# A decoder trunk on one core: when the attention units of a head pair are started beside the projections of the next pair

## The chip, the core and the metric

The kernel runs on one core of a Trainium2 chip. The metric is the device time of one execution in microseconds; for the kernel before three runs were timed, and one more execution was profiled. The names of the engines are those of the profile: PE (TensorE matmuls), PEld (its weight loads), DVE (VectorE), ACT (ScalarE), POOL (GpSimd), SP (SyncE, which issues all transfers spoken of here). One microsecond of TensorE's time is spent, in most of the kernel, on fp32 products made of three fp32r products each.

## What is computed

Two layers over 1024 tokens of width 1024 (float32): the first mixes tokens with a forgetting attention of 16 heads of 64, the second with a convolution, and each is followed by a gated feed-forward net of width 2816 with a short convolution. The change touches the attention of the first layer alone, which is, cut to its core:

```python
proj = h @ w_in                                   # q, k, v and one gate logit per head
log_f = jax.nn.log_sigmoid(proj[..., 3 * d:] + b_f)
cum = jnp.cumsum(log_f, axis=1)                   # per head, over tokens
q, k = rms_norm(q, q_g), rms_norm(k, k_g)         # over the 64 of a head
for i in range(s // 128):                         # causal
    logits = q[i] @ k[:i+1].T / sqrt(64) + cum[i][:, None] - cum[:i+1][None, :]
    p = softmax(where(kpos <= qpos, logits, -inf))
    out[i] = p @ v[:i+1]
x = x + concat(out) @ w_o
```

## The kernel before

The heads are worked through in 8 pairs, p = 0 to 7. For a pair, `project` (L801) runs over 8 blocks t of 128 tokens: 24 matmuls of 128x384 into a PSUM tile `pj` (two buffers), which give the block's q, k and v of both heads. `mm3` (L349 to L355) makes each product of three (hi by hi, lo by hi, hi by lo), from halves that `split` (L345) makes: the hi by a cast on ACT (L346), the lo by a subtraction on POOL, or DVE (L347). The block is then copied out (L816 and L819 on ACT, L820 on DVE, the last reader of `pj`), its sums of squares go through ACT, DVE (L826) and POOL (L169, L170), q and k are scaled (L831, DVE) and transposed on PE (`qkT`, L836). After each second block, a chunk of 256 tokens is split into sq, kd, kl (L842 to L851), and copies on SP's queue (L853) bring the halves to the other partitions. These tiles lie in a pool of 22 buffers, 16 of them for one pair.

A unit of attention is one head and one group g of 256 query tokens. Its first half (`softmax_rows`, L885) computes scores on PE (L897 to L900), adds the gate term and takes the minimum on DVE (L904), the exponential on ACT (L910), the reciprocal on DVE (L911) and the scaling on POOL (L912). Its second half (`weigh_values`, L916) transposes on PE (`pT`, L926), splits (ACT L933, DVE L934) and multiplies by v into `ov` (L938, L939), which ACT and DVE add up in `of` (L943, L944). When both heads of a group are through, `finish_unit` (L948) writes the 128 columns' hi and lo: straight into the operand of w_o if that lies in SBUF already (ACT L955 and DVE L956, on 128x128, twice), or else through `ohi` (ACT L960) and `olo` (POOL L961) and stores on SP (L966) to memory, from where `fetch` (L998) brings them back. `fetch(hf, k0, k1)` brings pairs k0 to k1-1 for the half hf of the tokens (512 each), and makes that half's operand tiles.

A pair has eight units; groups run from 3 down to 0 (short units last), in the last pair from 0 up to 3. `step()` takes the next unit from the list `pend`, writes its first half, and the second half of the unit before it. In the loop over pairs and blocks (L1013 to L1043) one `step()` follows each block, so that the units of pair p-1 lie beside the projections of pair p; the last pair's eight units follow when its projections are written. A fetch of the first half stands behind block 4 of the last pair. After the last pair the pool of the projection weights is closed, and `early` loads w_o: three slices of 512 KB into the space of that pool (`wohi`, `wolo`: L1049, L346, L347 of 128x1024), then three more into the pool of 22. Then comes the fetch of the second half, and the remaining units.

A scheduler behind the language moves instructions among each other, with priority by the order in which they are written; so the order on an engine is not that of the source, and each engine then works through its own order without skipping. The product with w_o (`attn_out`, L1064; PSUM tile `wops`) is moved in between the last units in this way.

Of the kernel before, what the change touches and what calls it, by code (L numbers as in the profile page):

```python
# [22 lines left out]
KT = D // P  # L23
# [6 lines left out]
def f32(ap):  # L30
    return ap.bitcast(F32)
# [17 lines left out]


N_POOL = 10
ROW_BUFS = 8
GATES = (2, 1)
BEAT = (3.3, 3.6)
# [58 lines left out]
class Trunk:  # L113
# [21 lines left out]
    def rows_to_cols(self, pool, psum, tag, dst, rows, later=None):  # L135
# [3 lines left out]
        tot = sum(r.shape[0] for r in rows)  # L139
        t = pool.tile([P, P], F32, tag="rows", name=self.n("rows"), bufs=ROW_BUFS)  # L140
        o = 0
# [561 lines left out]
    def attn(self, wst0, x_in, gain, w_in, b_f, q_g, k_g, extra=lambda *a: None, early=lambda: None):  # L703
        nc, tc = self.nc, self.tc
        W = 3 * P + NH
        with ExitStack() as st:
# [20 lines left out]
            def load_w(p, q):  # L727

                wid = W if p == 0 else 3 * P
                hi, lo, raw = (  # L730
                    wp.tile([P, 2 * W + 32], dt, tag=m, name=self.n(m), bufs=n)[:, : 2 * wid].rearrange(
                        "p (k n) -> p k n", k=2
                    )
                    for m, dt, n in (("whi", F32R, WIN_BUFS), ("wlo", F32R, WIN_BUFS), ("raw", F32, 2))
                )
                ks = slice(2 * q, 2 * q + 2)
                for j in range(2):
                    qkv = wv[:, 2 * q + j, : 3 * D].rearrange("p (s n) -> p s n", s=3)
                    nc.sync.dma_start(
                        raw[:, j, : 3 * P].rearrange("p (s n) -> p s n", s=3), qkv[:, :, p * P : (p + 1) * P]  # L740
                    )
                if p == 0:
                    nc.sync.dma_start(raw[:, :, 3 * P : W], wv[:, ks, 3 * D : 3 * D + NH])
                self.split(hi[:, :, :wid], lo[:, :, :wid], raw[:, :, :wid], p == 0)
                return hi, lo
# [33 lines left out]
            for a in range(2):  # L779
                t = cp.tile([P, 512], F32R, name=f"ptd{a}")  # L780
# [5 lines left out]
            def load_norm(t):  # L786
                xt = first[t] if t < 2 else load_x(t)
                self.norm_block(xp, pss, "s", xt, self.to_split_as_is(ht[t // 4]), t, "x", gains=[grow])
# [3 lines left out]
            def new_pair(p):  # L792
                pairs[p] = []
# [154 lines left out]
            def finish_unit(p, g, ofull):  # L948

                if g // 2 in ot:  # L950
                    for e in range(2):
                        i = 2 * g + 1 - e
                        c = slice((i % 4) * P, (i % 4 + 1) * P)
                        hi, lo = (m.at(p)[:, c] for m in ot[g // 2])
                        nc.scalar.copy(hi, ofull[:, e, :])  # L955
                        nc.vector.tensor_tensor(lo, ofull[:, e, :], f32(hi), op=ALU.subtract)  # L956
                else:
                    hi = sp.tile([P, 2, P], F32R, tag="ohi", name=self.n("ohi"), bufs=1)
                    lo = sp.tile([P, 2, P], F32R, tag="olo", name=self.n("olo"), bufs=1)
                    nc.scalar.copy(hi, ofull)  # L960
                    nc.gpsimd.tensor_tensor(lo, ofull, f32(hi), op=ALU.subtract)  # L961

                    for e in range(2):
                        i = 2 * g + 1 - e
                        for a, t in ((0, hi), (1, lo)):
                            nc.sync.dma_start(otd[a][p, :, i * P : (i + 1) * P], f32(t[:, e, :]))  # L966

            def attn_units(p):
                st = {}

                def first(g, h):
                    if h not in st:
                        nct = xp.tile([P, S], F32, tag="nct", name=self.n("nct"), bufs=NC_BUFS)
                        nc.sync.dma_start(nct, ncd[2 * p + h : 2 * p + h + 1, :].partition_broadcast(P))
                        st[h] = nct
                    st[g, h] = softmax_rows(p, h, g, st[h])

                def second(g, h):
                    if h == 0:
                        st["of", g] = sp.tile([P, 2, P], F32, tag="of", name=self.n("of"))  # L980
                    weigh_values(p, h, g, st[g, h], st["of", g])
                    if h == 1:
                        finish_unit(p, g, st["of", g])

                gs = range(4) if p == KT - 1 else range(3, -1, -1)
                return [(lambda g=g, h=h: first(g, h), lambda g=g, h=h: second(g, h)) for g in gs for h in range(2)]

            pend = []
            late = []

            def fetch(hf, k0, k1):

                if hf not in ot:
                    ot[hf] = self.ht_half(hf)
                for q in range(2):
                    j0, j1 = max(k0, 4 * q), min(k1, 4 * q + 4)
                    for a in range(2 if j0 < j1 else 0):
                        nc.sync.dma_start(  # L998
                            f32(ot[hf][a].q[q][:, j0 - 4 * q : j1 - 4 * q, :]),
                            otd[a][j0:j1, :, hf * 512 : (hf + 1) * 512].rearrange("k p s -> p k s"),  # L1000
                        )

            def step():

                if pend:
                    a, b = pend.pop(0)
                    a()
                    late.append(b)
                    if len(late) > 1:
                        late.pop(0)()  # L1010
                elif late:
                    late.pop(0)()

            for p in range(KT):
                if p == 0:
                    load_norm(0)
                ws = [load_w(p, q) for q in range(KT // 2)] if p else w_first + [load_w(0, q) for q in range(1, KT // 2)]
                new_pair(p)
                if p == 0:
                    load_norm(1)  # L1020
                for t in range(NB):
                    project(p, ws, t)
                    step()
                    if p == 0 and t + 2 < NB:
                        load_norm(t + 2)
                    if p == KT - 1 and t == 4:
                        fetch(0, 0, KT - 2)
                    if p == 0 and t == NB - 1:
                        tables = extra(sp, ptr, "tr")
                    if p == 1 and t >= 4:  # L1030
                        for _ in range(2):
                            if tables:
                                tables.pop(0)()
                if p == 0:
                    cum()
                pend += attn_units(p)
            wst.close()
            early()
            fetch(1, 0, KT - 2)
# [67 lines left out]
    def conv(self, xs, xd, h, ht, w_pw1, los, taps, vec, w_pw2, halo, after):  # L1107
# [4 lines left out]
        H = C - 1  # L1112
        n_pool = N_POOL
        wv = w_pw1.rearrange("(k p) n -> p k n", p=P)
# [475 lines left out]
```

## Time and profile before

| | us |
|---|---|
| three timed runs | 2339.28, 2334.06, 2335.76 |
| their median | 2335.76 |
| the profiled execution | 2333.51 |
| its span | 2331.8 |
| PE busy from 30 to 515 (projections with attention) | 474.33 of 485 |
| PE busy from 515 to 600 (the last units, first of w_o) | 75.44 of 85 |
| PE busy from 600 to 1000 | 394.00 of 400 |

The span is the time between the first and the last instruction of the profiled execution; the execution's own time is 1.71 us longer. In a row of a timeline, the bracket says how long the engine sat idle before and which instruction released it. In a table of stretches, the busy time of each engine stands with the number of its instructions, and PEclk is the clock granted to TensorE as a share of full speed.

### The profile page before, as it was taken

What the parts mean: (1) busy time and instruction counts of PE and PEld (TensorE: products, weight loads), DVE (VectorE), ACT (ScalarE), POOL (GpSimd) and SP (SyncE); (2) the same over time, 40 slices, a digit from 0 to 9 for tenths busy, and PEclk for the clock granted to TensorE, in tenths of its full rate; (3) what the DMA queues carried; (4) which work ended last, traced back from release to release, by engine and by line L of the source; (5) the groups of instructions that cost most, each with busy time, mean ns of one, the idle gap of its engine ahead of it and who ended that gap; (6) DMA issues with size and microseconds to landing.
All of it is one profiled execution on the core that took longest, in us unless ns stands there. A gap on an engine that the chain in (4) does not pass through costs nothing.

```text
span 2331.8 us, 35304 instructions
## 1 busy us (share of the span) xinstructions
PE 2253.5 (97%) x11282; PEld 1927.3 (83%) x11282; DVE 1650.9 (71%) x2751; ACT 1355.8 (58%) x2832; POOL 1403.7 (60%) x1188
## 2 busy tenths in 40 slices
PE   7899999998999999999999999998899999999998
PEld 7899999997878887777787887777687788888887
DVE  5567777777368999998436995699539999983322
ACT  5567667667255666666445665566535666664443
POOL 3355455535018988885554886677425999955453
PEclk9999999999999999999999999999999999999999
DMA  5222222144256456666888767664454455466664
GB/s 145 65 78 83 78 78 78 56 130 141 80 180 191 154 157 205 201 200 198 301 257 288 257 218 270 205 185 144 147 193 157 150 157 154 147 228 206 219 204 153
DMA packets 366841, 392.63 MB, mean 168 GB/s; under 512 B 26416, under 2 KB 245312, under 8 KB 366656
## 3 DMA queue, kind: packets, MB, share of 16 engines
q1 hardware_dynamic: 366656, 390.38, 52.8%
q8 instruction: 89, 1.46, 0.3%
q14 instruction: 96, 0.79, 0.1%
HBM read 299.78 MB, written 82.12 MB: 164 GB/s over the span
## 4 chain that ended last, share of the span: by engine, by line
PE 49%; DVE 15%; issue 4%; ACT 4%; DMA 2%; POOL 1%; SPq 0%; DVEq 0%; ACTq 0%; POOLq 0%
DVE acc L578 8%; PE dn L353 7%; PE dn L352 7%; PE dn L354 7%; PE pw L352 2%; PE pw L353 2%; PE pw L354 2%; PE y L352 2%; PE e L352 2%; PE e L354 2%; PE e L353 2%; PE y L353 2%; PE y L354 2%; ACT acc L582 1%; PE z L352 1%
## 5 line engine op out<-in xcount | busy, mean ns | idle before, releaser
L347 POOL TENSOR_TENSOR wlo<-raw,whi 128x512 fp32r<-128x512 f32 (+1 forms) x306 | 444.3, 1454 | 285.3 <-ACT whi L346 254.3
L346 ACT CAST whi<-raw 128x512 fp32r<-128x512 f32 (+2 forms) x497 | 303.2, 633 | 268.2 <-PE dn L353 154.8
L347 DVE TENSOR_TENSOR wlo<-raw,whi 128x512 fp32r<-128x512 f32 (+1 forms) x191 | 149.3, 785 | 229.8 <-ACT whi L346 214.3
L347 POOL TENSOR_TENSOR wlo<-s,whi 128x512 fp32r<-128x512 f32 x176 | 258.4, 1479 | 63.8 <-ACT whi L346 63.8
L352 PE MATMUL dn<-whi,whi 128*128 128x512 f32 x704 | 275.5, 391 | 1.2 <-ACT whi L346 0.7
L353 PE MATMUL dn<-wlo,whi 128*128 128x512 f32 x704 | 274.6, 390 | 0.8 <-POOL wlo L347 0.8
L354 PE MATMUL dn<-whi,wlo 128*128 128x512 f32 x704 | 274.4, 390 | 0.0
L1174 DVE SCALAR_TENSOR_TENSOR cacc<-u,ctaps,cacc 128x512 f32<-128x512 f32 x320 | 238.6, 754 | 9.0
L1179 POOL TENSOR_TENSOR pacc<-pacc,prod 128x512 f32<-128x512 f32 x144 | 188.7, 1313 | 50.3 <-ACT prod L1178 43.4
L352 PE MATMUL y<-bhi,whi 128*128 128x512 f32 x528 | 207.7, 393 | 7.6 <-DVE u L636 5.0
L354 PE MATMUL y<-bhi,wlo 128*128 128x512 f32 x528 | 205.7, 390 | 0.0
L353 PE MATMUL y<-blo,whi 128*128 128x512 f32 x528 | 205.6, 389 | 0.0
L169 POOL TENSOR_SCALAR ss<-ss 128x4 f32<-128x4 f32 (+1 forms) x96 | 22.6, 235 | 291.5 <-ACT hn L189 150.7
L352 PE MATMUL pj<-whi,hthi 128*128 128x384 f32 (+1 forms) x512 | 178.3, 349 | 5.1 <-DVE zf L822 1.9
L354 PE MATMUL pj<-whi,htlo 128*128 128x384 f32 (+1 forms) x512 | 177.9, 348 | 0.0
L353 PE MATMUL pj<-wlo,hthi 128*128 128x384 f32 (+1 forms) x512 | 176.8, 346 | 0.7 <-DVE wlo L347 0.7
L912 POOL TENSOR_SCALAR x<-x,nm 128x896 f32<-128x896 f32 (+7 forms) x128 | 101.0, 794 | 106.3 <-DVE nm L911 74.6
L556 POOL TENSOR_TENSOR s<-raw,raw 128x512 f32<-128x512 f32 x88 | 126.4, 1437 | 62.6 <-DMA c11d<-ev 57.4
L352 PEld LDWEIGHTS dn<-whi,whi 128*128 128x128 f32 x704 | 132.6, 188 | 29.5 <-ACT whi L346 1.2
L353 PEld LDWEIGHTS dn<-wlo,whi 128*128 128x128 f32 x704 | 132.4, 188 | 28.8 <-POOL wlo L347 1.2
L354 PEld LDWEIGHTS dn<-whi,wlo 128*128 128x128 f32 x704 | 132.4, 188 | 27.7
L582 ACT ACTIVATE acc<-acc 128x512 f32<-128x512 f32 x88 | 55.7, 633 | 164.3 <-DVE acc L578 163.0
(221 smaller groups left out, 6411.1 us busy)
## 6 DMA issues: line engine op xcount, KB each, us to landing
raw<-in_ffn_w_up_dram SPq DMA_DIRECT2D x240, 256.0 KB
raw<-in_ffn_w_down_dram SPq DMA_DIRECT2D x176, 256.0 KB
raw<-actd SPq DMA_DIRECT2D x152, 256.0 KB
raw<-in_conv_w_pw_dram SPq DMA_DIRECT2D x96, 256.0 KB
actd<-acc SPq DMA_DIRECT2D x76, 256.0 KB
wlo<-pwlo SPq DMA_DIRECT2D x64, 256.0 KB
raw<-in_fox_w_in_dram SPq DMA_DIRECT2D x64, 192.0 KB
xd<-x SPq DMA_DIRECT2D x24, 512.0 KB
```

The costliest lines, as they stand in the source:

```text
L169: nc.gpsimd.tensor_scalar(ss, ss, 1.0 / n, EPS, op0=ALU.mult, op1=ALU.add)
L346: self.nc.scalar.copy(hi, raw)
L347: (self.nc.vector if vector else self.nc.gpsimd).tensor_tensor(lo, raw, f32(hi), op=ALU.subtract)
L352: nc.tensor.matmul(out, lh, rh, start=start, stop=False, skip_group_check=more)
L353: nc.tensor.matmul(out, lh, rl, start=False, stop=False, skip_group_check=more)
L354: nc.tensor.matmul(out, ll, rh, start=False, stop=stop, skip_group_check=more)
L556: nc.gpsimd.tensor_tensor(st[o], *(st[m].rearrange("p a b -> p (a b)") if m[0] == "a" else st[m] for m in ((y, x) if o == "s4" else (x, y) ...
L578: nc.vector.scalar_tensor_tensor(acc[:, j:], ps[:, : 512 - j], tap[2 - j], acc[:, j:], op0=ALU.mult, op1=ALU.add)
L582: nc.scalar.activation(acc, acc, AF.Silu)
L912: nc.gpsimd.tensor_scalar(X[:, :L], X[:, :L], nm[:, 2:3], 1.0, op0=ALU.mult, op1=ALU.mult)
L1174: nc.vector.scalar_tensor_tensor(acc, win(j), tap(j), acc, op0=ALU.mult, op1=ALU.add)
L1179: nc.gpsimd.tensor_tensor(pacc, pacc, p, op=ALU.add)
```

## The change

A table `STEPS` says how many `step()` calls follow a block: none at blocks 0 and 1 of pair 1, two at its blocks 4 and 6, two at blocks 0 to 3 of the last pair, one elsewhere. So the eight units of pair 6 are written beside four blocks of pair 7. At block 4 of the last pair, its own units enter the list, and four of them (groups 0 and 1) follow blocks 4 to 7; four remain behind the projections. The fetch of the first half at block 4 now covers pairs 0 to 6, since pair 6 is written to memory altogether.

```diff
@@ -49,6 +49,7 @@
 N_POOL = 10
+STEPS = {(1, 0): 0, (1, 1): 0, (1, 4): 2, (1, 6): 2}
 ROW_BUFS = 8
@@ -1020,11 +1021,14 @@
                 for t in range(NB):
                     project(p, ws, t)
-                    step()
+                    if p == KT - 1 and t == 4:
+                        pend += attn_units(p)
+                    for _ in range(STEPS.get((p, t), 2 if p == KT - 1 and t < 4 else 1)):
+                        step()
                     if p == 0 and t + 2 < NB:
                         load_norm(t + 2)
                     if p == KT - 1 and t == 4:
-                        fetch(0, 0, KT - 2)
+                        fetch(0, 0, KT - 1)
@@ -1033,7 +1037,8 @@
                 if p == 0:
                     cum()
-                pend += attn_units(p)
+                if p < KT - 1:
+                    pend += attn_units(p)
             wst.close()
             early()
             fetch(1, 0, KT - 2)
```

Line numbers of the changed kernel are one higher from L53 on, and five higher from L1042 on (L347 becomes L348, L1049 becomes L1054).

What this does to the orders is shown at three places. The first is PE's order at the last pair's block 6 (`pj_7083` before, `pj_7250` in the change; `pj_6978` is the block before it; s are scores and pT transposes of pair 6). Before:

```order
L926 MATMUL pT_6701<-ident,x_6510 128x128
L353 MATMUL pj_6978<-wlo_6350,hthi_13_144 128x384
L354 MATMUL pj_6978<-whi_6349,htlo_15_146 128x384
L352 MATMUL pj_6978<-whi_6349,hthi_13_144 128x384
L353 MATMUL pj_6978<-wlo_6350,hthi_13_144 128x384
L354 MATMUL pj_6978<-whi_6349,htlo_15_146 128x384
L352 MATMUL pj_7083<-whi_6328,hthi_12_143 128x384
L353 MATMUL pj_7083<-wlo_6329,hthi_12_143 128x384
```

In the change:

```order
L927 MATMUL pT_6857<-ident,x_6691 128x128
L927 MATMUL pT_6857<-ident,x_6707 128x128
L898 MATMUL s_6990<-kd_5433,sq_5432 128x256
L899 MATMUL s_6990<-kl_5434,sq_5432 128x256
L901 LDWEIGHTS identb
L901 MATMUL s_6990<-maskt,identb 128x128
L353 MATMUL pj_7250<-whi_6328,hthi_12_143 128x384
L354 MATMUL pj_7250<-wlo_6329,hthi_12_143 128x384
```

Block 6 followed block 5's matmuls directly; in the change the 48 matmuls ahead of it (from the four transposes `qkT` of the second chunk on) are all of attention, and blocks 4 and 5 stand before those.

The second place is SP's order around the first loads of w_o (`raw`, from in_fox_w_o_dram). Before:

```order
L998 DMA hthi_1457_7308<-otd_103 128x4x512
L998 DMA htlo_1459_7310<-otd_104 128x4x512
L998 DMA hthi_1458_7309<-otd_103 128x2x512
L1049 DMA raw_7260<-in_fox_w_o_dram 128x1024
L1049 DMA raw_7266<-in_fox_w_o_dram 128x1024
L1049 DMA raw_7272<-in_fox_w_o_dram 128x1024
L998 DMA htlo_1460_7311<-otd_104 128x2x512
```

In the change (`kd_7067` and `kl_7068` are copies of the last pair's third chunk, `kd_7247` and `kl_7248` of its fourth):

```order
L854 DMA kd_7067<-kd_7067 64x256 x2
L1054 DMA raw_7435<-in_fox_w_o_dram 128x1024
L1054 DMA raw_7441<-in_fox_w_o_dram 128x1024
L854 DMA kl_7068<-kl_7068 64x256 x2
L1054 DMA raw_7447<-in_fox_w_o_dram 128x1024
...
L854 DMA kd_7247<-kd_7247 64x256 x2
L1054 DMA raw_7473<-in_fox_w_o_dram 128x1024
L967 DMA otd_104<-olo_7145 128x128 x2
L854 DMA kl_7248<-kl_7248 64x256 x2
L999 DMA htlo_1428_7155<-otd_104 128x3x512
L999 DMA hthi_1500_7483<-otd_103 128x4x512
```

The fetch of the second half stood ahead of w_o's loads and now stands behind five or six of them; the copies of the fourth chunk stand behind a store of pair 6's last `olo`.

The third place is POOL's order around the three `wolo` (the lower halves of w_o's first three slices). Before:

```order
L912 TENSOR_SCALAR x_7222<-x_7222,nm_7223 128x128
L912 TENSOR_SCALAR x_7232<-x_7232,nm_7233 128x256
L347 TENSOR_TENSOR wolo_7263<-raw_7260,wohi_7262 128x1024
L347 TENSOR_TENSOR wolo_7269<-raw_7266,wohi_7268 128x1024
L347 TENSOR_TENSOR wolo_7275<-raw_7272,wohi_7274 128x1024
L912 TENSOR_SCALAR x_7318<-x_7318,nm_7319 128x128
```

In the change (`ss_1463_7361` belongs to the last pair's block 7):

```order
L913 TENSOR_SCALAR x_7222<-x_7222,nm_7223 128x256
L348 TENSOR_TENSOR wolo_7438<-raw_7435,wohi_7437 128x1024
L170 TENSOR_SCALAR ss_1463_7361<-ss_1463_7361 128x4
L913 TENSOR_SCALAR x_7289<-x_7289,nm_7290 128x384
L962 TENSOR_TENSOR olo_7025<-of_6901,ohi_7024 128x256
L913 TENSOR_SCALAR x_7301<-x_7301,nm_7302 128x512
L348 TENSOR_TENSOR wolo_7444<-raw_7441,wohi_7443 128x1024
L171 TENSOR_TENSOR ss_1463_7361<-ss_1463_7361,mhalf 128x4
L913 TENSOR_SCALAR x_7380<-x_7380,nm_7381 128x384
L913 TENSOR_SCALAR x_7392<-x_7392,nm_7393 128x512
L348 TENSOR_TENSOR wolo_7450<-raw_7447,wohi_7449 128x1024
L962 TENSOR_TENSOR olo_7145<-of_7052,ohi_7144 128x256
```

The three `wolo` stood in a row; in the change block 7's sums of squares, normalisations and two `olo` stand between them.

## The prediction

> **What bounds the kernel now.** I read the page first, then a table of stretches around the end of attention, then TensorE's waits and the rows that hold them up. The page says that TensorE sets the time:
>
> ```profile
> span 2331.8 us, 35304 instructions
> PE 2253.5 (97%) x11282; PEld 1927.3 (83%) x11282; DVE 1650.9 (71%) x2751; ACT 1355.8 (58%) x2832; POOL 1403.7 (60%) x1188
> ```
>
> The profiled execution took 2333.51 us (1.71 us around the span); the median of the three runs, 2335.76, lies 2.25 above it, which is added at the end. About 78 us of the span are not TensorE's, so a change of order can win only where they lie. The table of stretches (columns: stretch, length, busy time of PE, PEld, DVE, ACT and POOL, granted clock, DMA share, GB/s):
>
> ```profile
> 90.00:100.00 10.00, 8.16 (x39) 7.40 (x38) 8.78 (x30) 7.45 (x17) 4.63 (x7) 0.67 0.10 26
> 450.00:520.00 70.00, 70.00 (x505) 69.06 (x504) 51.88 (x149) 47.34 (x122) 33.03 (x43) 1.00 0.36 108
> 520.00:530.00 10.00, 7.67 (x67) 6.99 (x65) 7.59 (x25) 9.08 (x24) 5.45 (x9) 1.00 1.03 401
> 530.00:540.00 10.00, 5.79 (x26) 4.37 (x25) 7.58 (x17) 5.28 (x16) 6.78 (x5) 0.86 0.82 269
> 537.00:541.00 4.00, 3.95 (x14) 3.38 (x15) 2.26 (x12) 2.30 (x9) 1.41 (x3) 0.57 0.90 307
> ```
>
> While the last pair is projected with one unit a block (450 to 520), TensorE has no gap: 505 matmuls in 70.00 us, 0.139 us each; I price TensorE's work of mixed attention and projection by that. From 520 to 540, behind the last projection, 6.54 us are lost: the short units of the old pair run in series and nothing else can go. The second place with a gap, 90 to 100, is the second pair's first blocks.
>
> ```profile
> PE ov L938 <- DVE of L944: 6.9, 4, 3.3
> 528.69 0.39 PE L938 MATMUL ov<-pthi,v 128*128 128x256 f32 x1 [2.33 <-DVE of L944]
> 531.61 0.39 PE L938 MATMUL ov<-ptd,v 128*128 128x256 f32 x1 [0.90 <-DVE of L944]
> 537.05 0.54 PE L938 MATMUL ov<-ptd,v 128*128 128x256 f32 x1 [3.32 <-DVE of L944]
> 532.19 3.89 DVE L956 TENSOR_TENSOR htlo<-of,hthi 128x128 fp32r<-128x128 f32 x2 [0.64 <-ACT hthi L955]
> 528.85 7.08 POOL L347 TENSOR_TENSOR wolo<-raw,wohi 128x1024 fp32r<-128x1024 f32 x3 [0.19 <-ACT wohi L346]
> L956 DVE TENSOR_TENSOR htlo<-of,hthi x12: 273/285/2423, 532.2 to 581.0; 128x128 fp32r<-128x128 f32 x12
> ```
>
> Three waits of TensorE for L944 make 2.33 + 0.90 + 3.32 = 6.55 us. The longest stands behind two L956 that took 3.89 us where one takes 0.285 (median), and they end just when POOL's three wolo end (528.85 + 7.08 = 535.93; L956 ends at 536.08). After that gap the clock was 0.57 in 537 to 541: (1 - 0.57) x 3.95 = 1.7 us.
>
> The Trainium skill ("SBUF — State Buffer", "SBUF: two separate sides") says that a VectorE instruction with two SBUF inputs and a GpSimd instruction exclude each other for a whole instruction; L956 is of that kind, and by this rule the trace agrees (2423 against 285 ns).
>
> **Part 1, the second pair's first blocks.** No unit is started beside blocks 0 and 1 of pair 1, and two at blocks 4 and 6. The scheduler had already put the matmuls of these blocks ahead of the first scores, so TensorE's order there is almost the same in both programs; what moves is one pair of transposes and one L831 of VectorE, now ahead of one L904 for which TensorE waits.
>
> ```profile
> 89.68 0.35 PE L897 MATMUL s<-kd,sq 128*128 128x256 f32 x1 [1.59 <-DVE nm L904]
> 96.35 0.38 PE L897 MATMUL s<-kd,sq 128*128 128x256 f32 x1 [1.83 <-DVE nm L904]
> L831 DVE TENSOR_TENSOR qk<-qk,ss x64: 399/426/2068, 30.1 to 522.9; 128x256 f32<-128x256 f32 x64
> ```
>
> One L831 is 0.43 us: I take +0.4; if the order helps instead, -0.4; if the next L904 is late as well, +0.8. That this part does nothing to the 1.83 us gap is therefore in the forecast.
>
> **Part 2, what goes from the old tail.** Pair 6's eight units are through by block 6 or so, and half of pair 7's stand amid its projections, so the three waits have other matmuls in them or no longer exist, and pair 6's two halves that went through L955 and L956 beside wolo are sent through memory. I take all of it as gone: 6.55 + 1.7 = 8.25 us. What takes its place follows.
>
> **Part 3, the stretch before block 6.** With two units a block, blocks 4 and 5 are used up as filler early, and 48 matmuls of attention alone now stand before block 6's first (in before, block 6 is interleaved). Block 6 needs the PSUM buffer of block 4, whose last reader is L820. In that stretch VectorE has ahead of it, with L820: two L934 of 512, one of 384, one L944, two L904 of 512 and two of 384 with four accumulator reads, three L911, two L847 and two L851, one L826.
>
> ```profile
> L934 DVE TENSOR_TENSOR ptlo<-pT,pthi 128x512 fp32r<-128x512 f32 x12 | 8.2, 685 | 0.9 <-ACT pthi L933 0.9
> L904 DVE CUSTOM_DVE_ANT_0 x<-s,nct 128x512 f32<-128x512 f32 x10 | 6.8, 684 | 2.6 <-PE s L898 2.5
> L934 DVE TENSOR_TENSOR ptd<-pT,ptd 128x384 fp32r<-128x384 f32 x8 | 4.4, 551 | 0.2 <-ACT ptd L933 0.2
> L847 DVE SCALAR_TENSOR_TENSOR sq<-qkT,asmall,sq 64x256 fp32r<-64x256 f32 x8 | 3.9, 483 | 0.9 <-ACT kd L843 0.7
> L851 DVE TENSOR_TENSOR kl<-qkT,kd 64x256 fp32r<-64x256 f32 x8 | 3.4, 422 | 0.2
> L944 DVE TENSOR_TENSOR of<-ov,of 64x256 f32<-64x256 f32 x8 | 3.4, 419 | 3.2 <-ACT of L943 3.1
> L826 DVE TENSOR_REDUCE ss<-sqr 128x4 f32<-128x256 f32 x7 | 2.9, 414 | 1.7 <-ACT sqr L824 1.6
> L911 DVE RECIPROCAL nm<-nm 128x1 f32<-128x1 f32 x14 | 2.1, 157 | 3.9 <-ACT x L910 3.9
> L820 DVE TENSOR_TENSOR v<-pj,v 128x128 fp32r<-128x128 f32 x7 | 1.9, 289 | 0.3 <-ACT v L819 0.2
> L904 DVE DVE_READ_ACCUMULATOR2_ANT nm<- 128x1 f32 x22 | 1.8, 82 | 0.0
> L904 DVE CUSTOM_DVE_ANT_0 x<-s,nct 128x384 f32<-128x384 f32 x2 | 1.1, 541 | 0.0
> ```
>
> 1.37 + 0.55 + 0.42 + 1.37 + 1.08 + 0.33 + 0.47 + 0.97 + 0.84 + 0.41 + 0.29 = 8.1 us. TensorE's 48 are 48 x 0.139 = 6.65. So TensorE waits 1.45 us. Bounds: 0, if VectorE is a few instructions ahead, as from 450 to 520 (51.88 of 70 busy); 2.0, if one more L904 of 384 lies in front.
>
> **Part 4, the first matmul of w_o.** In the order of the change, 41 matmuls stand between the last projection and the first wops, which needs w_o's first 512 KB, its cast on ScalarE (wohi), and for the third product wolo on POOL. These loads take the place of the closed weight pool, so they start when the last projection is through, in both programs.
>
> ```profile
> 519.22 0.34 PE L354 MATMUL pj<-whi,htlo 128*128 128x384 f32 x1
> 519.71 1.41 SPq L1049 DMA_DIRECT2D raw<-in_fox_w_o_dram  x3
> 527.73 1.04 ACT L346 CAST wohi<-raw 128x1024 fp32r<-128x1024 f32 x1
> 534.30 1.63 SPq L853 DMA_DIRECT2D kl<-kl  x2
> 84.83 0.81 SPq L974 DMA_DIRECT2D nct<-ncd  x2
> 88.84 0.69 DVE L904 CUSTOM_DVE_ANT_0 x<-s,nct 128x512 f32<-128x512 f32 x1 [1.24 <-DMA nct<-ncd]
> ```
>
> Before, the load left 0.15 us after the last projection ended (519.56) and was used 8.0 us after its issue, behind 2.5 MB of a fetch on the same queue. In the change the 3 MB fetch for the second half stands behind the w_o loads, and one pair of copies (1.63 us, as L853's) ahead of them. A 512 KB load in a quieter queue was used 4.0 us after issue (84.83 to 88.84). So the first wops can go at 0.15 + 1.63 + 4.0 + 1.04 = 6.8 us, TensorE is there at 41 x 0.139 = 5.7: 1.1 us. Eleven matmuls on, counted from the first wops (11 x 0.139 = 1.5 us), comes the product with wolo, and POOL must do an L912 of 256 and wolo first:
>
> ```profile
> L347 POOL TENSOR_TENSOR wolo<-raw,wohi 128x1024 fp32r<-128x1024 f32 x3 | 7.1, 2392 | 0.2 <-ACT wohi L346 0.2
> L912 POOL TENSOR_SCALAR x<-x,nm 128x512 f32<-128x512 f32 x3 | 2.1, 711 | 0.4 <-DVE nm L911 0.4
> L912 POOL TENSOR_SCALAR x<-x,nm 128x256 f32<-128x256 f32 x4 | 1.9, 479 | 4.8 <-DVE nm L911 4.7
> L912 POOL TENSOR_SCALAR x<-x,nm 128x384 f32<-128x384 f32 x3 | 1.8, 596 | 2.4 <-DVE nm L911 2.0 <-PE pT L926 0.4
> L170 POOL TENSOR_TENSOR ss<-ss,mhalf 128x4 f32<-128x4 f32 x1 | 1.0, 1010 | 0.1
> L961 POOL TENSOR_TENSOR olo<-of,ohi 128x256 fp32r<-128x256 f32 x1 | 0.7, 722 | 0.8 <-ACT ohi L960 0.8
> ```
>
> 0.48 + 2.39 - 1.5 = 1.3. Together 2.4 us; bounds 0 (the load lands early, and the L912 is done before it) and 6.4 (8.0 instead of 4.0).
>
> **Part 5, block 7 behind w_o.** The sum of squares of block 7 now passes L170 on POOL behind the second wolo. From the first wops: 2.87 (above) + 0.60 + 0.72 + 0.71 + 2.39 + 1.01 and 0.43 for L831 make 8.7 us, and TensorE comes to block 7's transposes after 2.87 + 44 x 0.139 = 9.0: hidden by 0.3, at no cost as long as TensorE's own work stands there. But the copies of that chunk's lower halves (kl) stand on SyncE's queue behind a store that needs the olo behind the third wolo: 8.3 (L170 ended) + 0.60 + 0.71 + 2.39 + 0.72 = 12.7, + 0.7 for issues, + landing. TensorE asks for them 85 matmuls after wolo, at 2.87 + 85 x 0.139 = 14.7 or somewhat later, as 18 of them are 512 wide. Landing in 4.0 gives 2.7 us of wait, in 1.3 none; 64 KB are less than 512, so I take 1.5, bounds 0 and 6.7 (landing 8.0). Before, the same copies were issued at 534.30, 14.7 us after the last projection, and nobody waited, since those units came last.
>
> **Part 6, the clock.** Around the two gaps of 1.59 and 1.83 us (Part 1) the clock was 0.67 over 10 us; so gaps of 1 to 1.5 us may cost some. I take 0.8, half of the 1.7 at 537 to 541; bounds 0 and 3.4 (two such places).
>
> The Trainium skill ("TensorE: Matmul & The Clock Gate", "What's actually happening") has the clock halved only after an idle window of about 3.4 us; the gap of 3.32 with 0.57 behind it agrees, the 0.67 around gaps of 1.59 and 1.83 does not fit it. By that rule Part 6 would be 0 and the time 0.8 lower.
>
> **Sum.** 0.4 + 1.45 + 2.4 + 0 + 1.5 + 0.8 = 6.55 us come, 8.25 go: -1.7. 2333.51 - 1.7 + 2.25 = 2334.1 us. The tail from 541 on (the fused units with w_o, then w_o alone) has the same work and I leave it.
>
> **The rivals.** A difference of 0.2% is 4.7 us, about what a measurement of this kernel can tell from no change; below 2331.1 is faster, above 2340.4 slower.
>
> All is hidden: VectorE is ahead in the stretch, w_o's loads land early, the copies too. Only Part 1 is left: 0.4 - 8.25 = -7.85, 2327.9 us. For it speaks that before block 6 VectorE was only 74% busy (51.88 of 70); against it, the fixed order of POOL and of SyncE's queue. Chance 0.28.
>
> Slower, by the landing of transfers: w_o's loads, the copies and the fetch crowd the queues (401 GB/s from 520 to 530, share 1.03), each lands late, and TensorE pays twice, at the first wops and at the last chunk's copies. With landing l beyond 4.0 us, the sum rises by 2l; it breaks even at l = 0.9. With 7.0 us, between the 4.0 and the 8.0 of the trace: Part 4 5.4, Part 5 4.5, clock 3.4, with 1.45 and 0.4 15.15 - 8.25 = +6.9, 2342.7 us. For it speaks the 8.0 of before; against it, that the large fetch is now behind. Chance 0.17.
>
> VectorE's instructions with two SBUF inputs meet wolo again: one L831 that starts inside a wolo (2.39 - 0.43 = 2.0 at most, and one in the trace did take 2068 ns), and L956 of pair 7 beside another load's lower half (1.0): +3.0, 2337.0 us. Chance 0.07.
>
> **How the numbers follow.** My forecast has 0.48, by itself 2331 to 2338. The three rivals reach from 2327.9 to 2342.7; 2327 to 2341 leaves out most of the slow one's upper half and little below. Faster: 0.28 and 0.04 of the forecast; slower: 0.17 and 0.01; within: the rest, 0.50.
>
> **What would show it.** Right: no wait of TensorE for L944 over 1 us behind the last projection, and no clock of 0.57 there; L956 near 0.3 us; a wait of some 1.5 us for L820 before block 6; a first wops some 7 us after the last projection with a wait for wohi, then one for wolo; scores of the last chunk that wait for a transfer; second pair as before. The prediction is wrong if the old waits for L944 return in other units, if the gaps of Parts 3 to 5 are missing (all hidden) or each beyond 3 us (the slow rival), or if the time moves in another stage.

## The result, and the profile after

The change is slower: 2348.22 us (median of six, 2341.36 to 2351.80) against 2337.03 us (six of the kernel before, 2334.06 to 2339.28), a ratio of 1.0046 with a 95% interval of 1.003 to 1.0062. That is 11.2 us more, outside the predicted range of 2327 to 2341 and on the side of the rival, but not by the rival's mechanism, as will be seen. The profiled execution took 2347.04 us. Its page:

```profile
span 2345.3 us, 35311 instructions
PE 2264.6 (97%) x11282; PEld 1933.3 (82%) x11282; DVE 1646.0 (70%) x2747; ACT 1354.8 (58%) x2830; POOL 1404.1 (60%) x1190
```

TensorE has the same 11282 matmuls, and is busy 11.1 us longer with them; its idle time grew by 2.4 us only. To find the place, I cut both traces where the same work is done: at ACT's copy of the first pair's last block, at its copy of the last pair's block 3, and at TensorE's 2.0 us wait for L1079 in w_o. Before, these lie at 64.1, 485.0 and 582.0 us; after, at 62.7, 490.9 and 591.7. The table of these stretches (stretch, length, busy time of PE, PEld, DVE, ACT and POOL, granted clock, DMA share, GB/s), before:

```profile
64.10:485.00 420.90, 413.03 (x2886) 404.94 (x2887) 296.07 (x860) 273.87 (x679) 205.38 (x252) 0.99 0.27 75
485.00:582.00 97.00, 87.45 (x621) 79.95 (x619) 74.99 (x216) 68.45 (x170) 45.26 (x52) 0.98 0.43 146
100.00:340.00 240.00, 239.39 (x1704) 235.19 (x1703) 169.71 (x493) 160.29 (x401) 122.45 (x150) 1.00 0.27 75
```

and after:

```profile
62.70:490.90 428.20, 416.97 (x2885) 406.68 (x2886) 293.28 (x860) 272.91 (x679) 203.91 (x252) 0.99 0.26 74
490.90:591.70 100.80, 91.00 (x622) 80.77 (x620) 74.18 (x212) 67.78 (x168) 46.50 (x54) 0.97 0.43 149
100.00:340.00 240.00, 235.17 (x1660) 228.85 (x1659) 161.99 (x476) 154.42 (x387) 114.56 (x143) 1.00 0.24 67
540.00:545.00 5.00, 4.50 (x18) 3.31 (x17) 4.77 (x12) 4.20 (x11) 4.72 (x6) 0.50 0.60 194
```

The same matmuls (2886 and 2885, 621 and 622) take 428.20 instead of 420.90 us in the first stretch, which I call the **pairs' stretch** (pairs 1 to 6 and the start of 7), and 100.80 instead of 97.00 in the second, the **last stretch** (the rest of pair 7, its units and the first products with w_o). That is 7.3 + 3.8 = 11.1 us, as much as the medians differ by. (The profiled executions differ by 13.5 us: ahead of both stretches the one after was 1.4 us faster, behind them 3.8 us slower.) Two thirds of the loss are where I had put 0.4 us.

TensorE's waits between 100 and 340 us show a part of it (engine, line, what it waited for: us in total, times, longest). Before:

```profile
PE ov L938 <- ACT ptd L933: 0.3, 1, 0.3
PE pT L926 <- DVE kl L851: 0.2, 1, 0.2
```

After, with line numbers one higher:

```profile
PE pT L927 <- DVE kl L852: 2.7, 4, 1.2
PE ov L939 <- ACT ptd L934: 1.1, 1, 1.1
PE s L898 <- DVE nm L905: 0.8, 2, 0.5
```

0.5 us of waits became 4.6, all of them small and far behind the four blocks that the table names. They fall beside the projections of pairs 2 to 4, from 166 to 315 us. The transposes pT wait for L852 because the tile of a chunk's own transposes, of which L852 is the last reader, shares three PSUM buffers with them.

In the last stretch, the old waits for L944 are gone (6.9 us before, one of 0.4 left), and these have come (beside them both traces have the wait of 2.0 us for L1079, now L1084, at which the stretches are cut):

```profile
PE s L898 <- DVE nm L905: 2.1, 4, 0.9
PE wops L355 <- DMA htlo<-otd: 1.5, 1, 1.5
PE s L899 <- DMA kl<-kl: 1.2, 1, 1.2
PE pT L927 <- DVE kl L852: 1.2, 3, 0.6
PE qkT L837 <- DVE qk L832: 0.5, 1, 0.5
PE ov L939 <- DVE of L945: 0.4, 1, 0.4
```

TensorE's idle time in the last stretch is 100.80 - 91.00 = 9.8 us, against 97.00 - 87.45 = 9.55 before: ten smaller waits (4 + 1 + 1 + 3 + 1 in the first five rows, 6.5 us) took the place of three (6.55 us). The slow clock, counted as in the prediction, cost 0.50 x 4.50 = 2.25 us from 540 to 545 and some 0.7 behind it, against 1.7 before; this is an estimate. And 97.00 - 9.55 - 1.7 = 85.75 us of matmuls became 100.80 - 9.8 - 3.0 = 88.0: the same matmuls, 2.25 us longer, with no wait shown.

### The profile page after: what moved, and what is told of

Read it like the earlier page. It is cut to its first block, busy times and chain, and to the rows that moved or that the text cites. A ratio compares the mean times of both kernels' runs of the same rounds, so it can differ in the third digit from the quotient of the medians.

```text
span 2345.3 us, 35311 instructions
## 1 busy us (share of the span) xinstructions
PE 2264.6 (97%) x11282; PEld 1933.3 (82%) x11282; DVE 1646.0 (70%) x2747; ACT 1354.8 (58%) x2830; POOL 1404.1 (60%) x1190
## 4 chain that ended last, share of the span: by engine, by line
PE 52%; DVE 12%; issue 4%; ACT 3%; DMA 3%; POOL 1%; SPq 0%; DVEq 0%; ACTq 0%; POOLq 0%
PE dn L354 7%; PE dn L353 7%; PE dn L355 7%; DVE acc L579 6%; PE y L353 2%; PE y L354 2%; PE pw L353 2%; PE pw L355 2%; PE pw L354 2%; PE y L355 2%; PE e L355 2%; PE e L353 2%; PE e L354 2%; PE z L353 2%; PE z L354 2%
## 5 line engine op out<-in xcount | busy, mean ns | idle before, releaser
L348 POOL TENSOR_TENSOR wlo<-raw,whi 128x512 fp32r<-128x512 f32 (+1 forms) x306 | 442.3, 1447 | 293.7 <-ACT whi L347 256.1
L347 ACT CAST whi<-raw 128x512 fp32r<-128x512 f32 (+2 forms) x497 | 303.3, 633 | 273.9 <-PE dn L354 154.9
L348 DVE TENSOR_TENSOR wlo<-raw,whi 128x512 fp32r<-128x512 f32 (+1 forms) x191 | 148.4, 780 | 232.6 <-ACT whi L347 217.2
L348 POOL TENSOR_TENSOR wlo<-s,whi 128x512 fp32r<-128x512 f32 x176 | 258.4, 1478 | 63.9 <-ACT whi L347 62.8
L913 POOL TENSOR_SCALAR x<-x,nm 128x896 f32<-128x896 f32 (+7 forms) x128 | 99.2, 779 | 137.0 <-DVE nm L912 112.9
```

Of the source, the lines that this page charges most:

```text
L347: self.nc.scalar.copy(hi, raw)
L348: (self.nc.vector if vector else self.nc.gpsimd).tensor_tensor(lo, raw, f32(hi), op=ALU.subtract)
L913: nc.gpsimd.tensor_scalar(X[:, :L], X[:, :L], nm[:, 2:3], 1.0, op0=ALU.mult, op1=ALU.mult)
```

## The experiments

Theory A, formed on this reading: the second pair's table moves the scheduler's order not for four blocks but for all of pairs 1 to 6, and that costs some 6 us there; the last pair's part costs the other 4. Rival B: what shows in pairs 1 to 6 is this one execution's, and the last pair's part costs all of it. Each diff is against the kernel named with it; the medians of the experiments are of 12 runs, and all intervals are 95%.

**The second pair's part alone** (against the kernel before):

```diff
+STEPS = {(1, 0): 0, (1, 1): 0, (1, 4): 2, (1, 6): 2}
...
                     project(p, ws, t)
-                    step()
+                    for _ in range(STEPS.get((p, t), 1)):
+                        step()
```

> Only the second pair's part of the change: no unit at blocks 0 and 1 of pair 1, two at blocks 4 and 6; the last pair is as before. On every engine the order is that of the whole change up to the last pair. Theory A (the second pair's table moves the whole order of pairs 1 to 6, and the waits that come with it in pairs 1 to 3 cost time): TensorE again waits some 4 to 6 us between 100 and 340 us, where before waited 0.6, and the time is 5 to 7 us over before (ratio 1.002 to 1.003). Rival B (the last pair costs all of it, and the 6 us by which the profiled execution was late from 300 to 480 us were that execution's own): within 1.5 us of before. My prediction had +0.4 us for this part.

Measured: 2341.14 us against 2336.54, ratio 1.0021 (1.0011 to 1.0032), 4.6 us over before: a little under the 5 to 7 us of Theory A, and more than the 1.5 us of Rival B. The profile of its stretches:

```profile
62.40:491.10 428.70, 417.23 (x2887) 406.74 (x2887) 293.52 (x860) 273.40 (x680) 204.06 (x252) 0.99 0.26 74
491.10:585.30 94.20, 87.81 (x621) 80.47 (x619) 73.17 (x216) 68.49 (x169) 46.16 (x52) 0.98 0.44 148
```

The pairs' stretch takes 428.70 us, as in the whole change (428.20), and the waits from 100 to 340 are those of the whole change to a tenth of a microsecond: 2.7, 1.1 and 0.9. They belong to the order, not to an execution. The last stretch, whose source is as before, is 2.8 us shorter than before: the scheduler gave it another order too, with a wait of 2.6 us for `wohi` and without the three for L944; so the part as a whole costs 4.6 us and not 7.

**The last pair's part alone** (against the change):

```diff
-STEPS = {(1, 0): 0, (1, 1): 0, (1, 4): 2, (1, 6): 2}
+STEPS = {}
```

> Only the last pair's part: two units a block at blocks 0 to 3 of the last pair, then its own units beside blocks 4 to 7; the second pair is as before. The order is that of before up to the last pair, and that of the whole change from there. Theory A: 3 to 5 us over before (ratio 1.0013 to 1.002), with the same waits as in the whole change: for L904 and the transposes around the last blocks, 1.2 us for the copies kl of the last chunk, 1.5 us for htlo from memory, and a clock near 0.84 over 20 us. Rival B: 10 to 12 us over before (ratio 1.0045). My prediction had -2.1 us for this part.

Measured: 2340.32 us, ratio 1.0016 (1.0005 to 1.0026), 3.8 us over before. Theory A again. Both parts cost, 4.6 and 3.8 us; their sum, 8.4, lies within the interval of the whole change (7.0 to 14.5 us). Its stretches:

```profile
65.80:485.30 419.50, 413.04 (x2887) 404.94 (x2887) 295.69 (x860) 273.96 (x679) 205.46 (x252) 0.99 0.27 75
485.30:585.60 100.30, 89.95 (x621) 79.77 (x619) 74.59 (x212) 68.12 (x168) 46.32 (x54) 0.98 0.44 151
```

The pairs' stretch is as before (419.50), the last stretch as in the whole change (100.30). Six further programs below keep before's order in the pairs' stretch and take 419.7 to 421.5 us there, so the 428.20 and 428.70 are well outside what one execution differs from another.

**Two units a block, but pair 7's own units behind its projections** (against the last pair's part alone):

```diff
-                    if p == KT - 1 and t == 4:
-                        pend += attn_units(p)
...
-                if p < KT - 1:
-                    pend += attn_units(p)
+                pend += attn_units(p)
```

> The last pair's part without its second half: two units a block at blocks 0 to 3 of the last pair, and its own eight units behind its projections. Pair 6 still goes through memory. If the last chunk's copies and block 7's late chain (they are needed early only because the own units stand amid the projections) are what costs, this is 1 to 3 us faster than the last pair's whole part, and the wait for kl is gone while that for htlo from memory stays. If it is rather the missing units behind the last projection that leave TensorE without other work, this one is 2 to 4 us slower than the last pair's whole part, with waits for L944 as before.

Measured: 2335.61 us, ratio 1.0000 (0.9989 to 1.0011): 4.7 us faster than the last pair's whole part, more than I had expected, though the two intervals just overlap, and as fast as before. Its last stretch, and two of its waits:

```profile
483.30:580.20 96.90, 87.90 (x622) 79.31 (x620) 74.27 (x212) 67.74 (x168) 45.92 (x54) 1.00 0.46 155
PE s L898 <- DVE nm L905: 3.1, 4, 1.4
PE qkT L837 <- DVE qk L832: 1.8, 2, 1.3
```

So the loss of the last pair's part comes with its own units amid the projections. Without them no transfer is waited for (kl is gone as expected, and htlo too, since w_o reaches it later); the waits for L905 and L832 stay, and are longer than in the last pair's whole part (2.1 and 0.9 us). Note the clock: 1.00, although TensorE waits here 1.4 and 1.3 us at a time.

**The second pair changed elsewhere.** Two other tables, against the kernel before, with the same loop as in the first experiment:

```diff
+STEPS = {(1, 0): 0, (1, 2): 2}
```

> A smaller form of the second pair's part: no unit at block 0 of pair 1, two at its block 2, all else as before. TensorE's order differs from before's from the second pair on for some 1870 rows, about four pairs, and is before's again behind them. Theory A in the form that any such shift of the order costs waits in pairs 1 to 3: 2 to 4 us over before. If it is the two idle blocks together with the doubled blocks 4 and 6 that do it: within 1.5 us of before.

Measured: 2342.70 us, ratio 1.0021 (1.0009 to 1.0033). One unit moved by two blocks costs as much as the whole table, within the intervals. Its trace says less:

```profile
62.60:487.70 425.10, 415.90 (x2886) 406.90 (x2887) 293.48 (x860) 274.54 (x680) 205.02 (x252) 0.99 0.26 74
```

In the pairs' stretch this is 4.2 us over before, about half of the table's 7.8, and the last stretch took the 97.0 us of before.

```diff
+STEPS = {(1, 5): 2, (1, 7): 0}
```

> The second pair changed in the other direction: two units at its block 5 and none at its block 7; the last pair as before. TensorE's order differs from before's for some 1090 rows and is before's again behind them. If any departure from the old order in the second pair costs (it leads the scheduler to an order with more waits), 2 to 5 us over before. If the cost comes from attention that is taken out of the first blocks, so that it is missing there and crowds later, this one has nothing of it: within 1.5 us of before.

Measured: 2338.52 us, ratio 1.0010 (0.9997 to 1.0024); not decided by the time alone. Its trace has the stretches

```profile
63.10:487.80 424.70, 416.47 (x2887) 408.39 (x2887) 294.72 (x860) 274.38 (x680) 205.93 (x252) 0.98 0.26 74
487.80:587.10 99.30, 89.25 (x622) 81.21 (x620) 74.95 (x216) 68.48 (x169) 45.30 (x51) 0.95 0.41 143
```

with 3.8 us over before in the pairs' stretch, where a unit is started earlier and not later. Of these, 0.4 us are idle time and 3.4 are longer matmuls, part of them at a slow clock (0.83 from 150 to 160 us, where before had 1.00), and 0.7 lie ahead of 141 us, where the two orders part. So this one trace speaks for the first reading, that taking attention out of the first blocks is not needed for a loss; that any departure from before's order costs is not shown. The last stretch shows how far one execution may be off: its order is that of before, and yet it took 99.3 us at a clock of 0.95.

**The queue behind olo** (against the last pair's part alone): the lower halves of pair 6 on VectorE.

```diff
-                    nc.gpsimd.tensor_tensor(lo, ofull, f32(hi), op=ALU.subtract)
+                    (nc.vector if p == KT - 2 else nc.gpsimd).tensor_tensor(lo, ofull, f32(hi), op=ALU.subtract)
```

> The last pair's part alone (second pair as before), but the lower halves olo of pair 6 are made on VectorE instead of POOL, so that neither their stores nor, behind them on SyncE's queue, the last chunk's copies kl and the fetch of htlo stand behind the third wolo. If the queue behind olo is what delays kl and htlo, the waits of TensorE of 1.3 us for kl and 1.5 us for htlo of the last pair's part alone go, and it is 1.5 to 3 us faster than that part alone (that was 2340.3). If these transfers are late for another reason (crowded queues), the waits stay and the time is the same within 1 us. An olo on VectorE has two inputs in SBUF and may itself stand up to 2.4 us behind a wolo; then the time is the same or worse, with a longer L962.

Measured: 2338.34 us, ratio 1.0008 (0.9997 to 1.0019), 2.0 us under the last pair's part with olo on POOL (whose interval overlaps). Its last stretch and olo's row (shortest, median and longest in ns):

```profile
483.70:582.30 98.60, 90.31 (x621) 81.07 (x619) 75.85 (x216) 67.83 (x167) 44.60 (x49) 0.97 0.45 153
L962 DVE TENSOR_TENSOR olo<-of,ohi x3: 403/408/1706, 520.4 to 542.9; 128x256 fp32r<-128x256 f32 x3
```

No wait for kl or htlo is left in it, so both were late by the queue behind olo, and not by crowded transfers. The price stands in the second row: one olo took 1706 ns where another took 408, as was to be feared beside wolo.

**wolo off POOL, in the kernel before:** the test of the reading on which the whole gain was to rest.

```diff
-            self.split(hi, lo, raw)
+            self.split(hi, lo, raw, True)
```

> The kernel before, but the lower halves wolo of w_o's first three slices are made on VectorE instead of POOL. If the 3.3 us wait behind the last projection comes from VectorE's L956 standing behind POOL's wolo (my reading, by which the change was to win), L956 takes 0.3 us here, the gap of 3.3 us and the slow clock behind it are gone, but VectorE has some 1.5 us for each wolo of its own: between 4 us faster than before and the same. If L956 was only late for its own inputs, it stays at 2 us or more and the gap stays.

Measured: 2333.81 us against 2336.38, ratio 0.9988 (0.9977 to 1.0000). The last stretch, and L956's durations:

```profile
482.20:574.50 92.30, 85.98 (x621) 78.94 (x619) 75.34 (x219) 68.30 (x169) 38.05 (x48) 1.00 0.45 152
530.30 0.48 DVE L956 TENSOR_TENSOR htlo<-of,hthi 128x128 fp32r<-128x128 f32 x2
L956 DVE TENSOR_TENSOR htlo<-of,hthi x12: 273/284/1019, 530.3 to 573.5; 128x128 fp32r<-128x128 f32 x12
```

The last stretch falls by 4.7 us, the two L956 that had taken 3.89 us take 0.48, and of the three waits for L944 only the first, 2.33 us, is left. So the waits of 0.90 and 3.32 us and the slow clock could be had by one word, without moving a unit. As a time the whole is 2.6 us, at the edge of what this measurement tells.

**wolo in halves on POOL, in the kernel before:**

```diff
-            self.split(hi, lo, raw)
+            self.nc.scalar.copy(hi, raw)
+            for o in (0, 512):
+                s = slice(o, o + 512)
+                self.nc.gpsimd.tensor_tensor(lo[:, s], raw[:, s], f32(hi[:, s]), op=ALU.subtract)
```

> The kernel before, but each wolo is made by two POOL instructions of 128x512 instead of one of 128x1024. If an L956 waits for the end of the POOL instruction that runs, whatever its length, its longest here is 1.3 to 1.6 us instead of 2.4, the 3.3 us gap shrinks by 1 to 2 us, and the time is 1 to 3 us under before. If L956 waits for the whole row of wolo (for its data, or for the three together), it stays at 2.4 and more, and the time at that of before.

Measured: 2335.09 us, ratio 0.9992 (0.9978 to 1.0005): by time not told from before. Its last stretch, 2.1 us shorter than before, and L956:

```profile
480.90:575.80 94.90, 87.89 (x621) 80.20 (x619) 74.36 (x216) 68.74 (x170) 45.56 (x55) 0.98 0.44 148
L956 DVE TENSOR_TENSOR htlo<-of,hthi x12: 273/288/1368, 528.1 to 574.8; 128x128 fp32r<-128x128 f32 x12
```

The longest L956 fell from 2423 to 1368 ns, with POOL's instructions half as wide (7.59 us for six, where three took 7.08): it waits for the end of the POOL instruction that runs, not for the row of them. TensorE's waits for L944 fell from 6.9 to 2.9 us. The trace agrees here too with the rule of the Trainium skill that the prediction named ("SBUF — State Buffer", "SBUF: two separate sides").

**Both last-pair forms with wolo on VectorE.** First the form without own units amid the projections (the third experiment), with the same edit as above:

> Two units a block at blocks 0 to 3 of the last pair, its own units behind its projections, and wolo on VectorE. With wolo on POOL this form had no L956 behind the last projection, but waits of 1.3 and 0.6 us for L831 (through L170 behind wolo) and of 1.4 and 0.8 us for L904. If POOL's queue is what held L170, the waits for L831 go; but VectorE, which holds the L904, now has 3.6 us of wolo more. Theory: the two cancel, the last stage within 1.5 us of that with wolo on POOL (96.9 us from the copy of the last pair's block 3 to the first wait for L1079). If VectorE is not the limit there, 2 to 4 us less, which would be as good as the kernel before with wolo on VectorE (2333.8).

Measured: 2336.45 us, ratio 0.9999 (0.9987 to 1.0010). The last stretch took 98.20 us, against 96.90 with wolo on POOL: no gain, as the first theory had it, but not by its mechanism. The waits for L832 are gone, and those for L905 did not grow (2.7 us, from 3.1); new are 1.5 us for POOL's L913 and 1.3 us for `hthi` from ACT. Then the last pair's whole part, with olo and wolo on VectorE:

> The whole last pair's part (its own units amid its projections) with olo of pair 6 and wolo both on VectorE, so that nothing of POOL's wolo stands ahead of L170, of the stores or of the copies kl. If POOL's queue is what spoils the last pair's part, the last stage falls from 98.6 us (olo on VectorE alone) to 94 or 95, under the 97.0 of before, and the time is 1 to 3 us under before. If it is the order itself (the stretch before block 6, and the same matmuls taking longer in it: 2.3 us without any wait shown), it stays at 97 to 99 and the time at or above before.

Measured: 2335.56 us, ratio 0.9989 (0.9978 to 0.9999). The two last stretches, in this order:

```profile
482.20:580.40 98.20, 87.65 (x622) 79.09 (x620) 75.06 (x215) 67.70 (x167) 41.83 (x50) 1.00 0.45 154
```

```profile
482.70:581.70 99.00, 88.28 (x622) 79.40 (x620) 76.85 (x219) 68.12 (x168) 37.58 (x47) 1.00 0.45 152
```

By the time, the last pair's part now stands a little under before, as one outcome had it; by the trace its last stretch is still 99.0 us, 2 us over before and 6.7 over before with wolo on VectorE, as the other had it. Since the stretch is where this edit acts, I go by the trace, though it is one execution: POOL's queue was not all that spoils the last pair's part. Its order keeps the 2.5 us of waits for L852 and L905 ahead of the first wops, which stand in the whole change as well. But this trace also has new waits, 1.8 us for the transfer of `hthi` and 1.6 us for lower halves of w_o that VectorE makes, so how much of the 99.0 us is the order's alone stays open.

By the time, the best two of all are the kernel before with wolo on VectorE (0.9988) and this last one (0.9989), and they are not told apart, nor from before with wolo in halves (0.9992); the first has much the shorter last stretch and the smaller edit.

## Why the prediction was wrong

**Part 1 failed, and with it the forecast.** The prediction took 0.4 us, from the statement that "TensorE's order there is almost the same in both programs". That is true of the second pair's first two blocks, and so is the rest of the reading there: the gap of 1.83 us is still 1.71 us long. But it says nothing of what follows. Row by row, TensorE's orders in the two traces agree for the first 353 matmuls, to 81 us, and then fall in step again only for the last 7554, from 572 us before and 582 after: between them lie nearly all of pairs 1 to 7, some 3400 matmuls, and I compared two places of them. The scheduler that reorders by priority carried the shift of four blocks on through six pairs. Measured: 7.3 us in the pairs' stretch, of which 3.4 are idle time (4.2 more from 100 to 340 us, a little less ahead of it) and 3.9 are longer matmuls (busy 416.97 against 413.03 for the same number). A part of the longer matmuls is not the order's: eight executions with before's order were busy between 413.0 and 414.5 us in this stretch, so that at least 2.5 us are left for the order. These I could not put down to a line, and their cause stays open. As a price by time, the part alone costs 4.6 us. One of the prediction's own signs of being wrong, "if the time moves in another stage", is what happened.

**Part 2 was right.** The three waits for L944 are gone with the change, and the experiments on wolo show that the two later ones were what I read them to be: L956 behind wolo on POOL, 2.4 us for each running instruction. What I did not ask is whether it needs a change of order at all to remove them.

**Parts 3 to 5: most places right, the sum a little too small** (5.35 us, where the ten waits make 6.5). The stretch before block 6 cost 0.36 + 0.69 = 1.05 us, for 1.45; the waits are for L852 and L905 of the same chain, not for L821. The first wops went 7.2 us after the last projection, where I had 6.8, but without a wait of its own, nor was there one for wolo, because waits for L852 and L905 (0.20, 0.90, 0.33) had made TensorE late in the 41 matmuls ahead of it. The five waits (the first two before block 6), then the transfers:

```profile
516.97 0.55 PE L927 MATMUL pT<-ident,x 128*128 128x128 f32 x3 [0.36 <-DVE kl L852]
518.21 0.38 PE L898 MATMUL s<-kd,sq 128*128 128x256 f32 x1 [0.69 <-DVE nm L905]
536.65 0.52 PE L927 MATMUL pT<-ident,x 128*128 128x128 f32 x3 [0.20 <-DVE kl L852]
538.07 0.39 PE L898 MATMUL s<-kd,sq 128*128 128x256 f32 x1 [0.90 <-DVE nm L905]
539.21 0.38 PE L898 MATMUL s<-kd,sq 128*128 128x256 f32 x1 [0.33 <-DVE nm L905]
534.59 1.04 SPq L1054 DMA_DIRECT2D raw<-in_fox_w_o_dram  x2
540.94 1.05 PE L353 MATMUL wops<-wohi,hthi 128*128 128x512 f32 x2
556.85 1.18 SPq L854 DMA_DIRECT2D kl<-kl  x2
560.84 0.39 PE L899 MATMUL s<-kl,sq 128*128 128x256 f32 x1 [1.22 <-DMA kl<-kl]
560.69 0.38 SPq L999 DMA_DIRECT2D htlo<-otd  x1
566.49 0.50 PE L355 MATMUL wops<-wo,htlo 128*128 128x512 f32 x1 [1.48 <-DMA htlo<-otd]
```

The copies kl left 15.9 us after the first wops (I had 13.4) and were used 4.0 us later: a wait of 1.22, for 1.5. So Part 5 was right in its place, and the experiment with olo on VectorE confirms that the chain passes olo on POOL, which stands behind the third wolo there. What it left out stands one row further down the same queue: the fetch of htlo, behind the same olo, 1.48 us. Block 7's chain, priced at nothing, cost 0.5 (L832).

**Part 6 was too small**: 3.0 us for 0.8, all around one place, 0.50 from 540 to 545. In the last pair's part alone, which has the same order (from 501 us of the change on) and nearly the same waits, the clock was 0.77 to 0.89 at that place; so this term is one execution's in part.

**A term was missing altogether**: 2.25 us for the same matmuls in another order, by the sum above. Two executions with a clock of 1.00 in the last stretch bear it out: it is busy 88.28 us in the last experiment and 85.98 us in the kernel before with wolo on VectorE, 2.3 us apart. I priced TensorE by 0.139 us a matmul on both sides and so took order to be free. Why the same matmuls take longer is not shown.

**The rival on the slow side** had the right sign by the wrong mechanism: w_o's load was used 4.1 us after its issue, as in the forecast, not 7, and TensorE did not wait for it. The third rival, two SBUF inputs beside POOL, shows in one L957 of 1380 ns and costs no wait. For the last stretch as a whole the forecast was -2.1 us, and +3.8 was measured; by the figures above, the 5.9 us between them are 1.45 of idle time, 2.2 of the clock and 2.25 of longer matmuls.

## What to carry to other kernels

Where a scheduler sets the order, compare the two orders over their whole length before calling a part of a change free: four table entries moved some 3400 matmuls, and the waits that came of it lay 50 to 240 us behind the blocks they named. Cut two traces at the same piece of work and compare the time and the busy time of equally many matmuls; that found in one view what no list of the longest waits shows. And when one instruction is the cause of a gap (here two lower halves that stand behind POOL's), move that instruction to another engine first; that took 4.7 us out of the stretch with one word (2.6 us by time, at the edge of the measurement), where the moved units took three waits away and made ten smaller ones.

## What the runs showed of the hardware

The waits of a given order come back to 0.1 us: 2.7, 1.1 and 0.8 us from 100 to 340 us in the change, 2.7, 1.1 and 0.9 in the program with the second pair's part alone, which has the same order there. The clock does not: at the same place of one order it was 0.50 from 540 to 545 us in one program and 0.77 from 535 to 540 in another, and with waits of 1.4 and 1.3 us it stayed at 1.00 in a third.

```profile
535.00:540.00 5.00, 4.58 (x21) 3.12 (x20) 4.15 (x11) 4.14 (x9) 4.72 (x6) 0.77 0.61 173
```

This row is of the last pair's part alone, at the stretch that answers to 540 to 545 of the change. VectorE's L956, with two inputs in SBUF, is done only when the POOL instruction that runs beside it is: it took 285 ns in the median, 2423 ns at most beside POOL's subtractions of 128x1024, and 1368 beside those of 128x512.
